# A transformer layer's ConvFFN: down projection as seven half-matrix products over all tokens, both up blocks in a row, convolution taps summed in PSUM

## The chip, the cores and the metric

The kernel runs on one core of one Trainium2 chip. The metric is the device time of one execution in microseconds (us). TensorE multiplies matrices into PSUM, VectorE (DVE), ScalarE (ACT) and GpSimd (POOL) work on vectors in SBUF, the first two also in PSUM, and SyncE (SP) mostly issues transfers. All data is float32. A matrix product is made of three TensorE passes over high and low parts of the operands (high x high, high x low, low x high), so each operand is first split: a cast gives the high part, a subtraction the low part.

## What is computed

One layer of a hybrid backbone over 2048 tokens and 256 context tokens with 1024 channels: a mixer (long convolutions, a state space scan, attention), an output projection with a norm, and then the part that the change touches, a gated feed-forward network with a short convolution along the tokens and a last norm:

```python
def _conv_ffn(h, w_up, conv_w, conv_b, w_down):
    u = _dwconv(h @ w_up, conv_w, conv_b)       # w_up: 1024 x 5632, three taps a channel
    g, val = jnp.split(u, 2, axis=-1)           # 2816 channels each
    return (jax.nn.silu(g) * val) @ w_down      # w_down: 2816 x 1024
...
x = _layernorm(ALPHA * x + gate * ffn, ln2_g, ln2_b)
```

## The kernel before

All engines run in order; the order on each engine is laid out by a scheduler when the kernel is built, which places instructions by their dependences and by estimated times. Transfers are issued from SP's queue (`nc.sync`), ScalarE's (`nc.scalar`) and GpSimd's (`nc.gpsimd`).

Everything up to the output projection is not touched, but for one thing: `outproj` takes its PSUM banks from the pool `ps_f`, of eight banks (one bank holds 128 x 512 numbers). It works through 16 tiles of 128 tokens, normalizes each, transposes it (`h2_tile`) and writes the seven input operands of the up projection (`operands`) to memory, or for the first two of them straight to SBUF.

`ffn` treats the tokens in two blocks e of 1024. For each block it runs 22 column tiles ct of the up projection, and then the down products of those token tiles that are complete.

*Up* (`up`, L1685 to L1725). The gate and value columns of a tile come from a 2 x 2 split of weights and tokens in seven products ("11", "t1", "t2", "t3", "21", "22", "t4") of twelve 128x512 matmuls each (`product`, L1657). VectorE adds the products out of PSUM into two tiles `ug` and `uv`. Three taps of the convolution follow on VectorE for each half: a scaling with bias (L1715) and two multiply-adds (L1717), all from SBUF to SBUF. ScalarE applies Silu to the gate half (L1721), VectorE multiplies the halves (L1723), and the result goes to the array `d_g[ct]` in memory. The operands stay in SBUF for a whole block in `bop`; those of the second block replace them piece by piece during the first down stage (`load_operands(1, ...)`, the iterator `side`).

*Down* (`down`, L1742 to L1770). Groups of three or four token tiles, two column halves each, so six or eight banks. For each of 22 channel tiles k the group loads its tokens from `d_g[k]`, splits them, takes the weights of row block k (two halves, split), and makes three matmuls for each tile and half (L1749 to L1751). In the second block the first eight channel tiles' weights are kept split in SBUF, in the place of the up operands. A finished tile is multiplied by the gate `g2` as it leaves PSUM (L1731), and the rest of it (`finish`, L1733: add the residual, norm, store) is put on a list `fins`, from which one is taken after each later step.

*Weights* (`weights`, L1580). One generator loads, combines and splits the weights of up and down in the order of their use, into a ring of six split operands. `split` casts on ScalarE (L1562) and subtracts in the helper `lo` (L481), mostly on GpSimd, sometimes on VectorE. `add` (L1592) combines weights on GpSimd. `take(n, more)` asks for the next n operands and prepares `more` ahead.

Of the kernel before, what the change touches and what calls it, by code (L numbers as in the profile page):

```python
# [9 lines left out]
F32 = mybir.dt.float32  # L10
# [7 lines left out]
P = 128  # L18
D = 1024
# [26 lines left out]
def shape_constants():  # L46
# [83 lines left out]
class SSD:  # L130
    """Both scans of the state space mixer, streamed over super-chunks of four chunks.  forward() yields after
    each piece of work, so that other work can be put between; the pieces of one super-chunk leave the forward
    part of y and the chunk states of the backward scan in memory, and backward() finishes from the last
    super-chunk to the first."""
# [39 lines left out]
    # step sizes and decays of chunks i0 .. i0 + n - 1  # L174
    def steps(self, i0, n):
# [7 lines left out]
        # softplus(x) = max(x, 0) + log1p(exp(-|x|))  # L183
# [17 lines left out]
        # inclusive sums within a chunk, forward heads then backward heads  # L201
# [76 lines left out]
    def off_diagonal(self, d, pr, at, hs, c_):  # L278
        """what the states hs give to the pair of heads pr over four chunks"""
# [12 lines left out]
    def rows(self, sc):  # L292
        """sums of the super-chunk as rows, split for the broadcasting products"""
# [9 lines left out]
    def forward(self, sc):  # L303
# [8 lines left out]
        # states: entering ones of the forward scan, own ones of the backward scan  # L312
# [153 lines left out]
class Build:  # L466
# [4 lines left out]
    def mm3(self, ps, pairs):  # L471
        """ps = sum over pairs of (wh, wl, xh, xl): wh.xh + wh.xl + wl.xh"""
# [23 lines left out]
    # work that runs between the pieces of other work  # L496
# [10 lines left out]
    # work that waits for a chain of other engines: run some pieces later  # L507
# [1356 lines left out]
```

## Time and profile before

| | us |
|---|---|
| median of 3 runs | 3097.09 (3082.59 to 3097.76) |
| span of the profiled execution, first to last instruction | 3087.5 |
| median less that span | 9.6 |
| output projection (from about 1500) | 213 |
| up, first block | 439.5 |
| down, first 7 token tiles | 222.5 |
| up, second block | 428.0 |
| down, last 9 token tiles | 274.5 |
| after the last matmul | 10.0 |

The stages are stretches of the profiled execution, cut where the first matmul of the next one starts; times inside it count from its first instruction. The profile lists no time of that execution other than its span, so the median of the runs is compared with the span.

### The profile page before, as it was taken

How to read it: one execution, taken by the hardware profiler on the slowest of the kernel's cores; microseconds unless marked ns; L12 is line 12 of the kernel's file. 1: busy time of each engine (PE TensorE's matmuls, PEld its weight loads, DVE VectorE, ACT ScalarE, POOL GpSimd, SP SyncE). 2: the span in 40 equal slices, each digit the busy share in tenths (PEclk: the TensorE clock that was granted, in tenths of full speed). 3: DMA queues.
4: the chain of work that ended last, by engine and by line, in shares of the span. 5: the costliest groups of instructions: out<-in, count | busy, mean ns of one | idle time of the engine just before them, and what ended most of it. 6: DMA issues, size and time to landing. Idle time of an engine off the chain costs nothing.

```text
span 3087.5 us, 41018 instructions
## 1 busy us (share of the span) xinstructions
PE 2920.1 (95%) x14153; PEld 2368.5 (77%) x14153; DVE 2198.1 (71%) x2924; ACT 1351.8 (44%) x2604; POOL 1772.2 (57%) x1418
## 2 busy tenths in 40 slices
PE   7899998899899898999999899999999999999998
PEld 4798696798866666666678788888778788888877
DVE  7953168642588977767678899999263999995344
ACT  7555135442367776667622323323333222223231
POOL 4644005300246656565564588987677899886463
PEclk9999999999999999999999999999999999999999
DMA  7467735343363329595556522223665222224563
GB/s 240 127 214 258 270 118 156 113 137 124 102 151 123 110 102 249 193 237 170 180 174 205 196 94 82 85 86 109 190 218 165 98 93 89 83 82 152 164 194 110
DMA packets 266546, 466.32 MB, mean 151 GB/s; under 512 B 32909, under 2 KB 153869, under 8 KB 262626
## 3 DMA queue, kind: packets, MB, share of 16 engines
q1 hardware_dynamic: 176656, 347.80, 36.7%
q10 hardware_dynamic: 84946, 100.55, 9.5%
q0 software_dynamic: 4736, 15.35, 1.4%
q8 instruction: 112, 1.84, 0.3%
q14 instruction: 96, 0.79, 0.1%
HBM read 325.97 MB, written 137.63 MB: 150 GB/s over the span
## 4 chain that ended last, share of the span: by engine, by line
PE 67%; DVE 13%; DMA 8%; issue 5%; ACT 4%; POOL 3%; ACTq 1%; SPq 0%; POOLq 0%; DVEq 0%
PE ps_f L1663 8%; PE ps_f L1662 8%; PE ps_f L1664 8%; PE ps_p L477 4%; PE ps_p L478 4%; PE ps_p L476 4%; PE ps_f L1750 3%; PE ps_f L1751 3%; PE ps_f L1749 3%; PE ps_f L476 2%; PE ps_f L477 2%; PE ps_f L478 2%; PE ps_o L1345 1%; PE ps_m L1305 1%; DMA kk<-d_ks 1%
## 5 line engine op out<-in xcount | busy, mean ns | idle before, releaser
L481 POOL TENSOR_TENSOR wrl<-wf,wrh 128x512 fp32r<-128x512 f32 x304 | 502.6, 1670 | 184.9 <-ACT wrh L1562 83.6
L481 POOL TENSOR_TENSOR pl<-pf,ph 128x512 fp32r<-128x512 f32 x186 | 263.3, 1424 | 197.1 <-ACT ph L1356 165.9
L1717 DVE SCALAR_TENSOR_TENSOR y<-u,cwf,y 128x1023 f32<-128x1023 f32 (+1 forms) x176 | 343.7, 1954 | 4.5
L1562 ACT CAST wrh<-wf 128x512 fp32r<-128x512 f32 x348 | 206.9, 618 | 240.7 <-PE ps_f L1663 139.5
L476 PE MATMUL ps_p<-hh,wh 128*128 128x342 f32 (+1 forms) x800 | 268.2, 335 | 0.0
L478 PE MATMUL ps_p<-hh,wl 128*128 128x342 f32 (+1 forms) x800 | 266.5, 334 | 0.0
L477 PE MATMUL ps_p<-hl,wh 128*128 128x342 f32 (+1 forms) x800 | 266.4, 333 | 0.0
L1306 DVE TENSOR_REDUCE mx<-ps_m 128x1 f32<-128x512 f32 (+1 forms) x320 | 196.1, 631 | 67.7 <-PE ps_m L1305 65.4
L481 DVE TENSOR_TENSOR wrl<-pc,wrh 128x384 fp32r<-128x384 f32 (+1 forms) x102 | 81.3, 799 | 211.4 <-ACT wrh L1616 200.8
L1562 ACT CAST wrh<-sw 128x512 fp32r<-128x512 f32 x132 | 81.2, 621 | 330.8 <-POOL sw L1592 230.4
L1750 PE MATMUL ps_f<-wrl,wrh 128*128 128x512 f32 x560 | 215.6, 394 | 5.4 <-POOL wrl L481 5.1
L1698 DVE TENSOR_TENSOR u<-ps_f,u 128x512 f32<-128x512 f32 x308 | 203.6, 684 | 17.2 <-PE ps_f L1664 11.7
L1751 PE MATMUL ps_f<-wrh,wrl 128*128 128x512 f32 x560 | 213.2, 390 | 1.9 <-DVE wrl L481 1.9
L1353 ACT ACTIVATE pf<-ps_s 128x512 f32<-128x512 f32 x288 | 168.2, 604 | 91.5 <-PE ps_s L1351 55.4
L481 DVE TENSOR_TENSOR wl<-wf,wh 128x1024 fp32r<-128x1024 f32 x36 | 48.4, 1343 | 223.5 <-ACT wh L834 223.4
L1356 ACT CAST ph<-pf 128x512 fp32r<-128x512 f32 x288 | 173.3, 629 | 20.1 <-DMA q<-d_qh 5.4
L239 POOL TENSOR_TENSOR hd<-h,dec 128x512 f32<-128x512 f32 x31 | 40.3, 1301 | 221.0 <-DVE h L248 141.3
L1749 PE MATMUL ps_f<-wrh 128*128 128x512 f32 x560 | 161.3, 390 | 0.5 <-ACT wrh L1562 0.5
L477 PEld LDWEIGHTS ps_p<-hl,wh 128*128 128x128 f32 x800 | 151.1, 189 | 11.7 <-issue 5.0
L478 PEld LDWEIGHTS ps_p<-hh,wl 128*128 128x128 f32 x800 | 150.6, 188 | 11.3 <-issue 5.0
L476 PEld LDWEIGHTS ps_p<-hh,wh 128*128 128x128 f32 x800 | 151.3, 189 | 8.8 <-issue 2.0
L1305 PE MATMUL ps_m<-k,q 128*128 128x512 f32 (+1 forms) x320 | 123.7, 400 | 14.8 <-DVE mx L1306 12.3
(475 smaller groups left out, 8718.9 us busy)
## 6 DMA issues: line engine op xcount, KB each, us to landing
wf<-in_ffn_w_down SPq DMA_DIRECT2D x94, 512.0 KB, 3.6
wf<-in_w_up SPq DMA_DIRECT2D x88, 512.0 KB, 3.5
wmod<-in_w_mod SPq DMA_DIRECT2D x24, 1024.0 KB, 7.5
wf<-in_w_col SPq DMA_DIRECT2D x36, 512.0 KB, 4.2
pc<-d_g SPq DMA_DIRECT2D x88, 192.0 KB, 3.3
kk<-d_ks SPq DMA_DIRECT2D x56, 256.0 KB, 8.9
d_g<-y SPq DMA_DIRECT2D x22, 512.5 KB, 2.6
d_g<-y SPq DMA_DIRECT2D x22, 511.5 KB, 2.7
```

Of the source, the lines that this page charges most:

```text
L476: mm(ps, lhsT=wh, rhs=xh, start=i == 0, stop=False)
L477: mm(ps, lhsT=wh, rhs=xl, start=False, stop=False)
L478: mm(ps, lhsT=wl, rhs=xh, start=False, stop=i == n - 1)
L481: eng.tensor_tensor(out=dst, in0=src, in1=hi.bitcast(F32), op=ALU.subtract)
L1562: self.nc.scalar.copy(w[0], x)
L1662: mm(ps, lhsT=w[0][:, js], rhs=b[0][:, j], start=j == 0, stop=False)
L1663: mm(ps, lhsT=w[0][:, js], rhs=b[1][:, j], start=False, stop=False)
L1664: mm(ps, lhsT=w[1][:, js], rhs=b[0][:, j], start=False, stop=j == 3)
L1717: v.scalar_tensor_tensor(y, u[:, o + k:o + k + n], cw[:, k, c:c + 1], y, op0=ALU.mult, op1=ALU.add)
L1749: mm(p, lhsT=x[0][:, ts], rhs=w[0], start=k == order[0], stop=False)
L1750: mm(p, lhsT=x[0][:, ts], rhs=w[1], start=False, stop=False)
L1751: mm(p, lhsT=x[1][:, ts], rhs=w[0], start=False, stop=k == order[-1])
```

## The change

The down projection waits until both blocks of up are done. It is then made over all 2048 tokens as seven products of half matrices: the tokens are split into two halves of 1024, the 2816 channels into two halves of 11 tiles (`KH`), the 1024 output columns into two halves of 512. A product covers eight tiles of 128 tokens (`PAIRS`), one bank each, and eleven steps k; each step needs one split weight piece of 512 columns and one split token piece of 1024. Sums and differences of pieces are formed as they are loaded. Those that are used again are stored: `d_gs` for tokens, `d_wt` for weights, both written in "t2". The last product, "t4", runs in three groups of three, three and two tiles and prepares its weights anew for each. The finishing of the first 1024 tokens is put on the list after "22", and taken from it in the steps of "t3"; that of the others after each group of "t4".

In up, the first tap of each half is made by ScalarE into a PSUM tile of two banks (`ps_c`, two such tiles), the other two taps are added there by VectorE, and Silu and the product read it. `ps_f` keeps four banks. A PSUM tile holds 1024 columns, so the last of the 1025 columns of the second block is done by itself. The operands of the second block are loaded after each product of the first block's last column tile.

```diff
-KEPT = 8
-DOWN = ((range(0, 4), range(4, 7)), (range(7, 10), range(10, 13), range(13, 16)))
+DOWN = ("11", "t2", "t1", "21", "22", "t3", "t4", "t4", "t4")
+PAIRS = (range(8), ) * 6 + (range(0, 3), range(3, 6), range(6, 8))
+KH = NFF // P // 2
...
-                self.ps_f = es.enter_context(tc.tile_pool(name="ps_f", bufs=8, space=PSUM))
                 self.ffn_start()
-                self.outproj()
-                self.ffn()
+                with tc.tile_pool(name="ps_f", bufs=4, space=PSUM) as self.ps_f:
+                    with tc.tile_pool(name="ps_c", bufs=2, space=PSUM) as self.ps_c:
+                        self.outproj()
+                        self.ffn_up()
+                self.ffn_down()
...
# weights()
-        def down(k, tiles, keep, first, last):
...
+        def down(name, k, last):
+            wd, h0, h1 = self.a["ffn_w_down"][0], slice(0, 512), slice(512, 1024)
+            r0, r1 = slice(k * P, (k + 1) * P), slice((KH + k) * P, (KH + k + 1) * P)
...
+            eng = g
+            if name == "11":
+                x = half(wd[r0, h0])
...
+            elif name == "t1":
+                x = half(self.d_wt[0][k])
+            elif name == "t2":
+                b1, x = raw(wd[r0, :]), half(wd[r1, h1])
+                add(b1[:, h1], b1[:, h1], b1[:, h0], ALU.subtract)
+                nc.sync.dma_start(self.d_wt[0][k], b1[:, h1])
+                add(x, x, b1[:, h1], ALU.subtract)
+                nc.sync.dma_start(self.d_wt[1][k], x)
+            elif name == "t3":
+                y, x = half(wd[r0, h1]), half(wd[r1, h1])
+                add(x, x, y, ALU.subtract)
+            else:
+                y, x = half(self.d_wt[1][k]), half(wd[r1, h0])
+                add(x, x, y, ALU.subtract)
+                eng = v if k % 2 else g
+            yield self.split(x, eng)
...
# up()
+                if e == 0 and ct == nf - 1:
+                    for _ in self.load_operands(1, [name]):
+                        pass
...
-                    v.tensor_scalar(y, u[:, o + 1:o + 1 + n], cw[:, 1, c:c + 1], cw[:, 3, c:c + 1], op0=ALU.mult, op1=ALU.add)
+            parts = ((0, 1023), ) if e == 0 else ((0, 1024), (1024, 1))
...
+                    if m > 1:
+                        y = self.ps_c.tile([P, 1024], F32, name="ps_c", tag="c")[:, :m]
+                    else:
+                        y = pool.tile([P, 1], F32, name="y1", tag=f"y1{i}")
+                    s.activation(y, u[:, o + 1 + p0:o + 1 + p0 + m], AF.Identity, scale=cw[:, 1, c:c + 1], bias=cw[:, 3, c:c + 1])
                     for k in (0, 2):
-                        v.scalar_tensor_tensor(y, u[:, o + k:o + k + n], cw[:, k, c:c + 1], y, op0=ALU.mult, op1=ALU.add)
+                        v.scalar_tensor_tensor(y, u[:, o + k + p0:o + k + p0 + m], cw[:, k, c:c + 1], y, op0=ALU.mult, op1=ALU.add)
...
+                s.activation(out[:, p0:p0 + m], ys[0], AF.Silu)
+                self.last = v.tensor_tensor(out=out[:, p0:p0 + m], in0=out[:, p0:p0 + m], in1=ys[1], op=ALU.mult)
...
+    def ffn_down(self):
...
+            def operands():
+                for n, name in enumerate(DOWN):
+                    c0, m = P * PAIRS[n][0], P * len(PAIRS[n])
+                    t1, t2 = slice(c0, c0 + m), slice(1024 + c0, 1024 + c0 + m)
+                    def load(src):
+                        x = self.pcpool.tile([P, 1028], F32, name="gr", tag="u", bufs=4)[:, :m]
+                        nc.sync.dma_start(x, src)
+                        return x
+                    for k in range(KH):
+                        lo_, hi_ = self.d_g[k], self.d_g[KH + k]
...
+                        elif name == "t1":
+                            x = load(self.d_gs[0][k])
+                        elif name == "t2":
+                            x, y, z = load(lo_[:, t2]), load(hi_[:, t2]), load(lo_[:, t1])
+                            v.tensor_tensor(out=x, in0=x, in1=y, op=ALU.add)
+                            nc.scalar.dma_start(self.d_gs[0][k], x)
+                            v.tensor_tensor(out=y, in0=x, in1=z, op=ALU.subtract)
+                            nc.scalar.dma_start(self.d_gs[1][k], y)
+                            x = y
+                        elif name == "22":
+                            x, y = load(hi_[:, t1]), load(self.d_gs[1][k])
+                            v.tensor_tensor(out=x, in0=x, in1=y, op=ALU.subtract)
+                        else:
+                            x, y = load(lo_[:, t1]), load(lo_[:, t2])
+                            v.tensor_tensor(out=x, in0=x, in1=y, op=ALU.subtract)
+                        w = [lp.tile([P, 1024], F32R, name="g" + e, bufs=4)[:, :m] for e in "hl"]
+                        s.copy(w[0], x)
+                        self.lo(v, w[1], x, w[0])
+                        yield w
...
+            def take():
+                while len(ops) < 3:
...
+            def evacuate(n, name, p, ps):
...
+                elif name == "22":
+                    add(xa[p][:, h1], xb[p][:, h1])
+                    fins.append(lambda: finish(p, xa[p], g))
+                elif name == "t3":
+                    add(xb[p][:, h1], xb[p][:, h1])
+                    add(xb[p][:, h0], xb[p][:, h0])
+                else:
+                    add(xb[p][:, h0], xb[p][:, h0])
+                    fins.append(lambda: finish(8 + p, xb[p], v if p > 5 else g))
+            def finish(t, r, eng):
+                x1 = lp.tile([P, D], F32, name="x1", bufs=2)
+                nc.sync.dma_start(x1, self.d_x1[t])
+                eng.tensor_tensor(out=r, in0=r, in1=g2, op=ALU.mult)
+                v.scalar_tensor_tensor(r, x1, ALPHA, r, op0=ALU.mult, op1=ALU.add)
+                self.norm(self.pcpool, r, gam, bet, r)
+                nc.scalar.dma_start(self.out[0, t * P:(t + 1) * P, :], r)
+            for n, name in enumerate(DOWN):
+                pairs = PAIRS[n]
+                ps = [ps_d.tile([P, 512], F32, name="ps_d", tag="d") for _ in pairs]
+                for k in range(KH):
+                    (w, ), x = self.take(1, 3), take()
+                    for i in range(len(pairs)):
+                        ts = slice(i * P, (i + 1) * P)
+                        mm(ps[i], lhsT=x[0][:, ts], rhs=w[0], start=k == 0, stop=False)
+                        mm(ps[i], lhsT=x[0][:, ts], rhs=w[1], start=False, stop=False)
+                        mm(ps[i], lhsT=x[1][:, ts], rhs=w[0], start=False, stop=k == KH - 1)
+                    if fins:
+                        fins.pop(0)()
+                for i, p in enumerate(pairs):
+                    evacuate(n, name, p, ps[i])
```

## Rows read from the trace of the kernel before

**Rows 1.** The page, part 1: busy time, share of the span, instructions.

```profile
PE 2920.1 (95%) x14153; PEld 2368.5 (77%) x14153; DVE 2198.1 (71%) x2924; ACT 1351.8 (44%) x2604; POOL 1772.2 (57%) x1418
```

**Rows 2.** Windows by stage: stretch, length, busy of each engine, clock, DMA, GB/s.

```profile
1713.00:2152.50 439.50, 428.74 (x1859) 350.18 (x1857) 419.88 (x387) 138.99 (x229) 358.84 (x276) 0.99 0.32 107
2152.50:2375.00 222.50, 216.46 (x930) 172.74 (x929) 93.56 (x107) 85.56 (x156) 151.13 (x109) 1.00 0.63 197
2375.00:2803.00 428.00, 422.98 (x1846) 346.11 (x1846) 412.17 (x372) 128.97 (x209) 380.94 (x293) 1.00 0.27 90
2803.00:3077.50 274.50, 272.65 (x1189) 222.22 (x1187) 114.92 (x157) 81.47 (x151) 135.68 (x100) 1.00 0.51 162
3077.50:3087.50 10.00, 0.14 (x1) 0.00 (x0) 4.92 (x7) 0.00 (x0) 1.46 (x1) 0.77 0.13 52
```

**Rows 3.** Windows of 50 us in the first up stage and the second down stage.

```profile
1700.00:1750.00 50.00, 43.41 (x185) 34.70 (x183) 38.28 (x56) 19.62 (x39) 20.97 (x21) 0.90 0.73 249
1750.00:1800.00 50.00, 46.67 (x205) 38.14 (x204) 49.25 (x44) 14.37 (x24) 37.35 (x30) 1.00 0.28 93
1950.00:2000.00 50.00, 50.00 (x220) 41.06 (x219) 48.88 (x44) 13.79 (x23) 46.28 (x34) 1.00 0.27 93
...
2900.00:2950.00 50.00, 50.00 (x220) 41.02 (x219) 16.94 (x28) 13.53 (x26) 22.40 (x17) 1.00 0.49 150
```

**Rows 4.** Timeline of VectorE, then of GpSimd, in the second up stage.

```profile
2616.52 3.52 DVE L1717 SCALAR_TENSOR_TENSOR y<-u,cwf,y 128x1025 f32<-128x1025 f32 x2
2620.14 2.14 DVE L1723 TENSOR_TENSOR y<-y 128x1025 f32<-128x1025 f32 x1
...
2604.63 1.29 POOL L481 TENSOR_TENSOR wrl<-sw,wrh 128x512 fp32r<-128x512 f32 x1
...
2616.84 4.35 POOL L481 TENSOR_TENSOR wrl<-wf,wrh 128x512 fp32r<-128x512 f32 x2 [1.01 <-ACT wrh L1562]
2621.14 1.18 POOL L1693 COPY u<-tail 128x2 f32<-128x2 f32 x1
```

**Rows 5.** Groups by line and shape, whole span: busy, mean ns of one, idle before.

```profile
L1698 DVE TENSOR_TENSOR u<-ps_f,u 128x512 f32<-128x512 f32 x308 | 203.6, 684 | 17.2 <-PE ps_f L1664 11.7
L1717 DVE SCALAR_TENSOR_TENSOR y<-u,cwf,y 128x1025 f32<-128x1025 f32 x88 | 168.9, 1921 | 2.2
L372 DVE SCALAR_TENSOR_TENSOR y<-xT,ssdc,ps_y 128x512 f32<-128x512 f32 x16 | 11.9, 745 | 7.1 <-PE ps_y L365 7.1
...
L481 POOL TENSOR_TENSOR fxl<-fax,fxh 128x1024 fp32r<-128x1024 f32 x15 | 38.2, 2545 | 12.4 <-ACT fxh L1072 6.3 <-PE ps_x L478 3.8 <-DMA d_xt<-tst 1.2
...
L1721 ACT ACTIVATE y<-y 128x1025 f32<-128x1025 f32 x22 | 23.4, 1065 | 46.9 <-DVE y L1717 46.9
```

**Rows 6.** Timeline after the last matmul: the last tile's norm.

```profile
3079.12 0.69 DVE L1427 BATCH_NORM_STATS2 bst<-r 128x6 f32<-128x512 f32 x1
...
3080.17 1.27 DVE L1434 SCALAR_TENSOR_TENSOR r<-r,bmv,gam 128x1024 f32<-128x1024 f32 x1
3080.39 1.46 POOL L1433 TENSOR_TENSOR brs<-bve,mhalf 128x1 f32<-128x1 f32 x1 [9.64 <-DVE bve L1431]
3081.89 1.28 DVE L1435 SCALAR_TENSOR_TENSOR r<-r,brs,bet 128x1024 f32<-128x1024 f32 x1 [0.45 <-POOL brs L1433]
```

**Rows 7.** Windows with the highest transfer rates; columns as in rows 2.

```profile
0.00:20.00 20.00, 11.08 (x27) 3.09 (x27) 7.77 (x19) 10.53 (x16) 7.38 (x19) 0.91 0.89 321
1720.00:1730.00 10.00, 5.24 (x12) 3.48 (x12) 7.75 (x10) 3.83 (x9) 5.26 (x5) 0.66 0.93 353
2300.00:2310.00 10.00, 6.62 (x28) 4.52 (x27) 9.68 (x12) 3.98 (x8) 7.57 (x5) 1.00 0.79 278
```

**Rows 8.** Timeline of the output projection: transposes, last evacuation, next transposes.

```profile
1618.07 1.04 PE L485 MATMUL ps_f<-ident,r 128*128 128x128 f32 x8
...
1624.86 0.46 ACT L1451 ACTIVATE h2t<-ps_f,mc 128x128 f32<-128x128 f32 x1 [0.39 <-DVE h2t L1454]
...
1629.85 1.04 PE L485 MATMUL ps_f<-ident,r 128*128 128x128 f32 x8
```

More of the change, by code (lines that the diff above doesn't have):

```diff
@@ L1638, in weights @@
                 yield from up(ct)
-            for n, tiles in enumerate(DOWN[e]):
-                for k in self.down_order(e, n):
-                    yield from down(k, tiles, e == 1 and k < KEPT, n == 0, n == len(DOWN[e]) - 1)
+        for n, name in enumerate(DOWN):
+            for k in range(KH):
+                yield from down(name, k, n == len(DOWN) - 1)
     def piece(self):
@@ L1733, in finish @@
-            def finish(t, r):
-                for b in range(2):
-                    bs = slice(b * 512, (b + 1) * 512)
-                    x1 = self.piece()
-                    nc.sync.dma_start(x1, self.d_x1[t][:, bs])
-                    v.scalar_tensor_tensor(r[:, bs], x1, ALPHA, r[:, bs], op0=ALU.mult, op1=ALU.add)
-                self.norm(pool, r, gam, bet, r)
-                nc.scalar.dma_start(self.out[0, t * P:(t + 1) * P, :], r)
-            def down(e, n, side):
-                tiles = DOWN[e][n]
-                nt, order = len(tiles), self.down_order(e, n)
-                ps = {(i, b): self.psf() for i in range(nt) for b in range(2)}
-                def products(i, b, k, x, w):
-                    mm, p, ts = nc.tensor.matmul, ps[i, b], slice(i * P, (i + 1) * P)
-                    mm(p, lhsT=x[0][:, ts], rhs=w[0], start=k == order[0], stop=False)
-                    mm(p, lhsT=x[0][:, ts], rhs=w[1], start=False, stop=False)
-                    mm(p, lhsT=x[1][:, ts], rhs=w[0], start=False, stop=k == order[-1])
-                ks = order[:nf - KEPT] if e == 1 and n == len(DOWN[1]) - 1 else order
-                for k in ks:
-                    x, *w = self.take(3, 3)
-                    for i in range(nt):
-                        for b in range(2):
-                            products(i, b, k, x, w[b])
-                    next(side, None)
@@ new lines, in ffn_up @@
+        first_operands(("21", "22", "t4"), bpool3)
+        for e in range(2):
+            for ct in range(nf):
+                for _ in first.pop(0) if first else up(e, ct):
+                    pass
+                if e == 0 and ct == 2:
+                    with tc.issue_after(self.last.ins):
+                        self.norm2 = [self.bc_row(pool, a["ln2_g"], "gam2"), self.bc_row(pool, a["ln2_b"], "bet2"),
+                                      self.bc_row(pool, self.d_mod[1:2, :], "g2")]
@@ L1772, in ffn @@
-            rs = {}
-            fins = []
-            first_operands(("t2", "t3"), bpool)
-            first = [up(0, 0), up(0, 1)]
-            next(first[0])
-            self.flush()
-            next(first[1])
-            self.oppool.release()
-            first_operands(("21", "22", "t4"), es.enter_context(tc.tile_pool(name="ffb3", bufs=1)))
-            for e in range(2):
-                for ct in range(nf):
-                    for _ in first.pop(0) if first else up(e, ct):
-                        if fins:
-                            fins.pop(0)()
-                    if e == 0 and ct == 2:
-                        with tc.issue_after(self.last.ins):
-                            gam = self.bc_row(pool, a["ln2_g"], "gam2")
-                            bet = self.bc_row(pool, a["ln2_b"], "bet2")
-                            g2 = self.bc_row(pool, self.d_mod[1:2, :], "g2")
-                side = self.load_operands(1, OPERANDS) if e == 0 else iter(())
-                for n in range(len(DOWN[e])):
-                    down(e, n, side)
-                for _ in side:
-                    pass
+                for i, p in enumerate(pairs):
+                    evacuate(n, name, p, ps[i])
```

173 lines of the change are left out of this document (99 added, 74 removed).

## The prediction

> **What bounds the kernel now.** I read the page first, then the windows by stage, then single stretches. The busy line of the page [rows 1] names the tensor engine, at 95% of the span. The windows by stage [rows 2] say where this is strictly so. In both up stages and in the second down stage it is busy for 98 to 99% of the time; in the first down stage it loses some 6 us. Full windows [rows 3] hold 220 matmuls in 50 us at clock 1.00, so one 128x512 matmul is issued every 0.2273 us (its listed 0.39 us overlaps its neighbours). Per stage that gives: the up products, 2 x 22 x 7 x 12 = 3696 matmuls, need 840 us and took 439.5 + 428 = 867.5; the down products, 16 x 2 x 22 x 3 = 2112, need 480 us and took 222.5 + 274.5 = 497, and 10 us of tail come after them, 507 in all.
>
> The second bound stands close behind it. In the up stages VectorE is busy 412 to 420 us and GpSimd 359 to 381 [rows 2], but these busy times hold waits for each other. In [rows 4] VectorE starts two convolution taps at 2616.52 and a multiply at 2620.14, and GpSimd two subtractions at 2616.84 and a copy at 2621.14. Alone, a tap takes some 1.28 us and such a subtraction 1.29 [rows 4, 6]. Together the three VectorE and two GpSimd operations take 5.76 us, from 2616.52 to 2622.28, which is 3 x 1.1 + 2 x 1.25: they take turns. So I count each VectorE operation with two SBUF inputs (1.1 us per 1024 columns, 0.55 per 512) and each GpSimd one (1.25 per 512) on one shared resource, "the turn". In the up stage one column tile needs 9 x 1.25 on GpSimd and 5 x 1.1 + 4 x 0.55 on VectorE (the two scaling operations at half price), 18.95 us, beside 84 x 0.2273 = 19.1 us of matmuls. That it fits shows that the turn can be nearly full.
>
> The Trainium skill (page "SBUF — State Buffer", section "Who interferes with whom") has this as an exclusive lock between GpSimd and VectorE instructions with two SBUF inputs, and says that a VectorE instruction with at most one SBUF input does not contend. The trace agrees on the first in [rows 4]; for the second, the adds out of PSUM stay at 684 ns while GpSimd is busy [rows 5]. By this rule the second part of the change helps VectorE, and the rest of the change, which gives both engines more two-input work, is hurt.
>
> **The change part by part.**
>
> *Fewer matmuls.* Seven half products: 7 x 8 x 11 x 3 = 1848 matmuls, 264 fewer, 60.0 us at 0.2273. 420 us remain.
>
> *Convolution taps in PSUM.* The first tap of each half goes from VectorE to ScalarE (one of 1025 columns costs 1.06 there [rows 5]), and the other four read one SBUF and one PSUM input. The nearest row is 745 ns for 512 columns with one PSUM input [rows 5], so some 1.28 for 1024; no row shows a write to PSUM, and 1.92, the present price, is the upper bound. VectorE falls from 18.9 to some 13.5 us a column tile, or 16.2 at the bound, and the turn to 12.4. Both are under 19.1, so all that can be won is what the matmuls lose today: 27 us over both stages. The windows [rows 3] put some 10 us of it before 1800, at the start, with operand loads and a clock of 0.90 that stay. I take 435 for the first block. One-column leftovers in the second block are small and stand under cover.
>
> *Four banks instead of eight.* The output projection shares the four. Its transposes at 1618.07 are evacuated by 1625.3, and the next ones, which would need the same banks, come at 1629.85 [rows 8]: 4 us to spare, cost 0 (up to 5 if VectorE falls behind). In the up stage four products are 10.9 us of cover against a conv burst of some 6.5.
>
> *Both up blocks in a row.* The 28 operand pieces of the second block, until now hidden in down, load within the last column tile of the first: 28 x 0.26 + 1.05 MB = 8.4 MB in 19 us, 440 GB/s, where the best 10 us window moved 353 [rows 7]; 24 us at that rate. I take 8 us (0 to 20). The second block: 428. Up 863, 4.5 less than now.
>
> *Into down.* All eight banks are wanted, four of them are the convolution's, which ends some 6 us after the last product; the matmuls reach the fifth bank after 2.7 us. 4 us (0 to 8).
>
> *The seven products.* Each step k has 24 matmuls, 5.45 us; a product, 60.0. "11", "t1", "21" and "22" put at most 1.31 MB (240 GB/s) and 3.5 us of turns on a step, so 60 each, 240 in all.
>
> *"t2", transfers.* A step loads three pieces of 0.524 MB, stores two, loads 0.79 MB of weights and stores 0.52: 3.93 MB, 43.3 MB in eleven steps. In 60 us that would be 720 GB/s, twice anything in [rows 7]. Read ahead ends at three operands, about 16 us or 5.5 MB. The rest at 353 GB/s is 107 us, and the last piece still needs a subtraction, a cast, a split and its matmuls, 10 us: 117. At 321, the best of 20 us, it is 128. Only four raw buffers serve three pieces a step, so the third load waits for the split of the step before; that chain (split 2.5, load 4, subtraction 1.3, waits) is 9 us a step, just under the 10.3 of the transfers, and on top of them in part would make 13 a step, 143: my upper end. The turn, 3 x 1.1 + 3 x 1.25, is 7.05 a step and hidden. The stores of the weight differences stand in SP's queue and wait for GpSimd's subtractions, with the next loads behind them; those of the token sums stand in ScalarE's queue and wait for VectorE, with the next casts behind. Both delays are part of that chain.
>
> The Trainium skill's page "DMA: Bandwidth & Descriptors" (section "Specifications") gives a fabric ceiling of 435 GB/s. By that figure this product would take 97 us, an estimate, and the sum would be 20 less; no row here comes near the rate, so the row stands.
>
> *"t3" and "t4", turns.* A step of "t3" has a subtraction and a split of 1024 on VectorE and of 512 on GpSimd, 4.7 us; eight finishing chains fall into it. Each now multiplies by the gate on GpSimd (1024 columns, 2545 ns in [rows 5]; alone on the turn 2.5) where today the evacuation did it out of PSUM, and has three full-width VectorE passes, 3.3: 5.8 us of turn. 11 x 4.7 + 8 x 5.8 = 98 us against 60 of matmuls. "t4" runs in three groups that prepare the same eleven weights each time: 1.25 + 0.93 + 0.42 = 2.6 us a step (2.46 in the last), 84 us (0.93 is the mean of six splits on GpSimd and five of 0.55 on VectorE, 0.42 the tokens' split of 384 columns), and six chains, 35: 119 against 60. Then two chains in a row on VectorE, each 1.28 x 3 for multiply and residual and first norm pass, 1.4 of statistics, 1.28 at the end [rows 6], and the store: 19 us where today's tail is 10. Together 236. At the lower bound the turns are free and VectorE's own time counts: in "t3" 22 passes of 1.22, 16 adds out of PSUM of 0.684 and eight chains of 5.6 (three passes, statistics 1.4, small ones 0.4), 83; in "t4" splits 27, adds 5.5, chains 34, 67; 83 + 67 + 19 = 169. At the upper, a tenth of the turns is lost in waits: 258.
>
> **Sum.** Down 4 + 240 + 117 + 236 = 597 against 507, +90; up -4.5. The profiled span of 3087.5 becomes 3173; the median of the runs is 9.6 above that span, so 3183.
>
> **Rivals.** (1) *The tensor engine sets the pace*, the other side. For it: the second down stage loses under 5 us in 274 [rows 2, 3] with nine finishing chains and all splits beside it. Against it: its matmul step had a third of the side work. Down is then 4 + 420 + 19, the time 3097 - 64 - 4.5 = 3029. It decides once the waits in "t2", "t3" and "t4" together, 57 + 97 in my sum, fall under 70. (2) *Turns are mostly hidden*: the lower bound 169 in the last two products, everything else as summed: 3116. (3) *Chains add up*: "t2" at 143, a tenth lost in turns, and the clock, which fell to 0.66 in a window with 5.2 us of matmuls in 10 but stayed 1.00 with 6.6 [rows 7], falls where matmuls pause, at some 10 us: 3097 + 85.5 + 26 + 22 + 10 = 3240.
>
> **Chances.** My forecast, between 3145 and 3215: 0.58. Rival 1: 0.08. Rival 2, 3100 to 3145: 0.14, a fifth of it within 0.5%. Rival 3: 0.20. About 0.5% (15 us) is what a measurement of this kernel can tell from no change. Faster 0.08, same 0.05 with the edges, slower 0.87. The range, 3112 to 3250, leaves out rival 1 and the top of rival 3.
>
> **What would show it.** Right: matmuls at 19.1 us a column tile in up, VectorE at some 70% there; in "t2" the matmuls half idle, behind a split that waits for a load, with over 300 GB/s; in the last two products both VectorE and GpSimd over 85% busy, and taps near 1.3 us. Wrong: "t2" near 60 us; GpSimd's 1024-wide multiply beside VectorE's passes without either stretching; or an up stage that the four banks hold above 19.5 us a tile.

## The result, and the profile after

The changed kernel takes 3206.7 us (median of 4 runs, 3200.55 to 3216.45) where the kernel before takes 3093.4 in the runs beside it: ratio 1.0375, 95% interval 1.0344 to 1.0405. It is slower by 113 us; the prediction was 3183, range 3112 to 3250. The profiled execution's span went from 3087.5 to 3198.7 us.

The page, part 1, for the changed kernel (the same line as [rows 1]):

```profile
PE 2917.5 (91%) x13889; PEld 2349.9 (73%) x13889; DVE 2137.2 (67%) x3004; ACT 1463.5 (46%) x2666; POOL 1584.2 (50%) x1394
```

The tensor engine has 264 instructions fewer, and yet its busy time fell by only 2.6 us. Its granted clock is 0.86, 0.87 and 0.76 in the windows of "t2", "t3" and "t4" below, a mix of its two levels (1.2 and 2.4 GHz), and each of these stretches holds long waits; where it has no waits, as in "t1", the clock is 1.00. No engine has more to do than before, but for ScalarE. So the time went into waits, and the windows by stage show where. They are cut at the first matmul of each step: output projection, first up block, second up block, the entry into down, "11", "t2", "t1", "21", "22", "t3", "t4", tail. Columns as in [rows 2].

```profile
1510.90:1717.30 206.40, 192.14 (x897) 159.66 (x895) 154.12 (x211) 51.44 (x90) 108.06 (x88) 0.96 0.53 181
1717.30:2159.30 442.00, 430.38 (x1859) 351.09 (x1858) 295.94 (x347) 198.13 (x280) 276.49 (x287) 0.99 0.32 108
2159.30:2593.00 433.70, 426.88 (x1849) 347.98 (x1847) 337.80 (x425) 205.93 (x324) 274.40 (x291) 0.99 0.27 91
2593.00:2604.80 11.80, 0.19 (x1) 0.01 (x1) 11.10 (x12) 6.77 (x8) 1.27 (x1) 0.73 0.87 291
2604.80:2666.90 62.10, 61.97 (x265) 50.84 (x265) 17.79 (x14) 15.54 (x22) 27.79 (x20) 0.97 0.74 259
2666.90:2767.20 100.30, 73.42 (x265) 56.62 (x265) 39.61 (x31) 22.33 (x31) 36.87 (x24) 0.86 0.96 352
2767.20:2827.20 60.00, 60.00 (x265) 49.68 (x266) 21.94 (x25) 17.15 (x23) 19.82 (x11) 1.00 0.50 168
2827.20:2892.20 65.00, 59.95 (x265) 49.35 (x264) 22.18 (x20) 18.76 (x24) 20.14 (x12) 1.00 0.47 159
2892.20:2959.30 67.10, 61.64 (x264) 50.59 (x264) 34.39 (x30) 16.30 (x21) 21.49 (x15) 0.96 0.68 231
2959.30:3054.90 95.60, 72.56 (x264) 56.49 (x265) 94.86 (x87) 16.89 (x24) 76.74 (x38) 0.87 0.66 230
3054.90:3181.50 126.60, 86.66 (x264) 56.40 (x264) 96.05 (x106) 28.47 (x56) 85.13 (x53) 0.76 0.60 196
3181.50:3198.70 17.20, 0.35 (x2) 0.00 (x0) 13.27 (x18) 0.00 (x0) 2.78 (x2) 0.62 0.15 61
```

Each product has the same 264 matmuls and could be done in 60.0 us; only "t1" is. "t2" has the transfer engines taken for 0.96 of its time, "t3" has VectorE busy for 99% of it, and in "t4" no engine is above 76%. Against the sum of the prediction, term by term in us:

| term | predicted | measured | difference |
|---|---|---|---|
| output projection (four banks) | 0 | 197.0 before, 205.3 after | +8.3 |
| up, first block, second block with the transition | 435 + 428 | 442 + 434 | +13 |
| into down | 4 | 11.8 | +7.8 |
| "11", "t1", "21", "22" | 240 | 62.1 + 60.0 + 65.0 + 67.1 = 254 | +14 |
| "t2" | 117 | 100.3 | -17 |
| "t3" | 98 | 95.6 | -2 |
| "t4" | 119 | 126.6 | +8 |
| tail | 19 | 17.2 | -2 |

These differences sum to +30; the work ahead of the output projection ended 4 us earlier in the profiled execution after, and the two make the 26 between the 3173 summed and the 3198.7 found. (The output projection's times run from the start of its first product to the start of its last, without the transposes that follow.)

### The profile page after: what moved, and what is told of

It is laid out like the page before. It is cut to its first block, busy times and chain, and to the rows that moved or that the text cites. A ratio compares the mean times of both kernels' runs of the same rounds, so it can differ in the third digit from the quotient of the medians.

```text
span 3198.7 us, 40745 instructions
## 1 busy us (share of the span) xinstructions
PE 2917.5 (91%) x13889; PEld 2349.9 (73%) x13889; DVE 2137.2 (67%) x3004; ACT 1463.5 (46%) x2666; POOL 1584.2 (50%) x1394
## 4 chain that ended last, share of the span: by engine, by line
PE 64%; DVE 13%; DMA 11%; issue 5%; POOL 3%; ACT 3%; SPq 0%; ACTq 0%; DVEq 0%; POOLq 0%
PE ps_f L1679 8%; PE ps_f L1678 8%; PE ps_f L1680 8%; PE ps_p L479 4%; PE ps_p L478 4%; PE ps_p L477 4%; DMA gr<-d_g 2%; DMA wf<-in_ffn_w_down 2%; PE ps_f L478 2%; PE ps_f L477 2%; PE ps_f L479 2%; DMA kk<-d_ks 2%; PE ps_d L1883 2%; PE ps_d L1884 2%; PE ps_o L1350 1%
## 5 line engine op out<-in xcount | busy, mean ns | idle before, releaser
L482 POOL TENSOR_TENSOR wrl<-wf,wrh 128x512 fp32r<-128x512 f32 x216 | 308.4, 1428 | 400.0 <-ACT wrh L1563 379.3
L1882 PE MATMUL ps_d<-wrh,gh 128*128 128x512 f32 x616 | 256.1, 427 | 73.8 <-ACT gh L1827 30.8
L1883 PE MATMUL ps_d<-wrl,gh 128*128 128x512 f32 x616 | 260.5, 423 | 23.2 <-DVE wrl L482 12.4
L1751 DVE SCALAR_TENSOR_TENSOR ps_c<-u,cwf,ps_c 128x1023 f32<-128x1023 f32 (+1 forms) x176 | 224.3, 1285 | 58.5 <-ACT ps_c L1749 57.0
L1884 PE MATMUL ps_d<-wrh,gl 128*128 128x512 f32 x616 | 235.3, 407 | 15.1 <-DVE gl L482 9.2
L1827 ACT CAST gh<-gr 128x1024 fp32r<-128x1024 f32 (+2 forms) x99 | 84.4, 858 | 303.0 <-PE ps_d L1883 175.5
L1882 PEld LDWEIGHTS ps_d<-wrh,gh 128*128 128x128 f32 x616 | 125.4, 207 | 115.6 <-ACT gh L1827 40.0
L1593 POOL TENSOR_TENSOR wf<-wf 128x512 f32<-128x512 f32 x110 | 162.4, 1476 | 92.6 <-DMA wf<-in_ffn_w_down 74.7
L482 DVE TENSOR_TENSOR gl<-gr,gh 128x1024 fp32r<-128x1024 f32 (+2 forms) x99 | 127.2, 1292 | 117.1 <-ACT gh L1827 117.1
L1883 PEld LDWEIGHTS ps_d<-wrl,gh 128*128 128x128 f32 x616 | 126.6, 206 | 60.7 <-DVE wrl L482 17.2
```

The lines of the kernel that those rows point to most:

```text
L482: eng.tensor_tensor(out=dst, in0=src, in1=hi.bitcast(F32), op=ALU.subtract)
L1751: v.scalar_tensor_tensor(y, u[:, o + k + p0:o + k + p0 + m], cw[:, k, c:c + 1], y, op0=ALU.mult, op1=ALU.add)
L1882: mm(ps[i], lhsT=x[0][:, ts], rhs=w[0], start=k == 0, stop=False)
L1883: mm(ps[i], lhsT=x[0][:, ts], rhs=w[1], start=False, stop=False)
L1884: mm(ps[i], lhsT=x[1][:, ts], rhs=w[0], start=False, stop=k == KH - 1)
```

## The experiments

Runs for which no ratio is given were executed once. The four executions of the changed kernel lie 16 us apart, so such runs are read by their stages, which repeat better: in the seven runs that leave "t2" as it is, it takes 99.6 to 103.8 us.

### What sets the pace of "t2": bytes or the four raw buffers

**Six raw buffers.** Every third load goes to a buffer of a second pair.

```diff
-x = self.pcpool.tile([P, 1028], F32, name="gr", tag="u", bufs=4)[:, :m]
+turn[0] += 1
+if turn[0] % 3:
+    x = self.pcpool.tile([P, 1028], F32, name="gr", tag="u", bufs=4)[:, :m]
+else:
+    x = lp.tile([P, 1024], F32, name="gr2", bufs=2)[:, :m]
```

> The changed kernel with six raw token buffers in the down stage where it has four (every third load goes to a buffer of a second pair), so that the loads of a step needn't wait for the split of the step before. In the changed kernel the second product, t2, takes 100.3 us at 376 to 378 GB/s. If the chain load, split, next load sets its pace, it falls by 15 to 20 us, to 80 to 85 (the turn's own floor is 77), and the whole to about 3185. If the transfers set it, as the prediction has it (43 MB at the rate that the queues reach), t2 stays within 4 us of 100 and the whole within 6 of 3204.

**No stores.** The changed kernel without the four stores of "t2".

```diff
-nc.sync.dma_start(self.d_wt[0][k], b1[:, h1])
...
-nc.sync.dma_start(self.d_wt[1][k], x)
...
-nc.scalar.dma_start(self.d_gs[0][k], x)
...
-nc.scalar.dma_start(self.d_gs[1][k], y)
```

> The changed kernel without the four stores of the second product (token sums, token differences, two halves of weight differences); the later products read other arrays of the same size instead, so their operands are not those of the reference. A step of t2 then moves 2.36 MB where it moved 3.93. If the bytes set t2's pace, it falls from 100.3 us to the larger of the turn (11 x 7.05 = 77) and the bytes at 376 GB/s (69): about 77, and the whole to about 3181. If the chain of four raw buffers sets it, it stays above 92. Products t1, 21 and 22 stay at 60, 65 and 67 under either.

**Both together.**

> The changed kernel with six raw token buffers (t2 81.8 us in the run six_raw, with 404 to 418 GB/s) and without the four stores of t2 (68.3 in the run no_stores; later products read other arrays, so their operands are not the reference's). Products 11 and t2 together took 162.4 in the changed kernel, 144.3 with six buffers, 136.2 without stores. If the 144.3 are set by bytes, taking away 17 MB of 43 brings t2 near its matmuls: 60 to 66, 11 and t2 together 122 to 128. If the turn (77 us of VectorE and GpSimd work) sets them, t2 stays at 72 to 78 and the two together above 133.

Six buffers: 3183.7 us, "t2" 81.8, where the theory of the chain said 80 to 85. No stores: 3182.3, "t2" 68.3, below what either theory said; "11" took 67.9 in that run, the two together 136.2. Both: 3161.4, "t2" 59.8, the two together 122.1. (The expectations' 376 to 378 GB/s is the rate over 82 us from 2654.5 on; over "t2" itself it is 352.) Windows of 10 us in "t2" of the changed kernel, which show that the queues are full at first and not at the end:

```profile
2660.00:2670.00 10.00, 9.89 (x44) 7.84 (x44) 2.85 (x3) 5.94 (x11) 5.59 (x4) 1.00 1.03 406
2700.00:2710.00 10.00, 7.95 (x23) 6.31 (x24) 4.25 (x4) 1.66 (x2) 5.16 (x4) 0.66 1.03 406
2730.00:2740.00 10.00, 7.19 (x31) 5.29 (x29) 4.13 (x4) 1.57 (x2) 1.81 (x1) 1.00 0.85 299
```

"t2" as one window, with six buffers:

```profile
2670.00:2752.00 82.00, 68.94 (x267) 54.63 (x266) 34.16 (x27) 20.05 (x26) 38.49 (x25) 0.90 1.03 412
```

and with six buffers and no stores:

```profile
2668.00:2728.00 60.00, 60.00 (x266) 49.70 (x265) 48.19 (x28) 20.37 (x29) 45.44 (x25) 1.00 0.96 339
```

With six buffers the queues run at 412 GB/s through the whole product; with four they fall to 299 in its second half. So neither theory was whole. Of the 40 us over the matmuls, 18 belong to the chain through four raw buffers (100.3 - 81.8), and 22 to the stores (81.8 - 59.8), 17 of the 43 MB. In the other order the shares differ: without the stores the chain costs 14, "11" and "t2" taken together, 5.7 of them a wait for the first bank of "t2". The edit also takes the stores' waits out of SP's and ScalarE's queues, so that the 22 are bytes alone is not shown; the steady 412 GB/s speaks for it. In the last run "t2" stands at its matmuls although the prediction counts 77 us of turns for it. That is no proof against turns: in this window lie 27 passes of VectorE with two SBUF inputs and 25 operations of GpSimd, 61 us at the prediction's prices, and seven of the 22 additions and subtractions of "t2" were done in "11".

### What sets the pace of "t3": the finishing chains and their turns

**No gate.** The gate multiply of each chain is left out.

```diff
-eng.tensor_tensor(out=r, in0=r, in1=g2, op=ALU.mult)
```

> The changed kernel without the multiplication by the gate in the finishing of a tile (the output lacks the gate). Fourteen of the sixteen are GpSimd operations over 1024 columns, eight of them in t3. Theory of turns (GpSimd and two-input VectorE work exclude each other): taking GpSimd work away speeds VectorE, which does not do it, by 2.5 us each: t3 falls from 95.6 us by 15 to 20, t4 and the tail together from 141.6 by 15 to 20, the whole to about 3170. Rival, VectorE's own work alone sets the pace: its passes stay as long as they are, t3 stays within 5 us, and the whole falls by less than 8 us, of which 3 are the last two tiles, gated on VectorE.

**No finishing chains of the first half.** The raw sums are stored.

```diff
-fins.append(lambda: finish(p, xa[p], g))
+nc.scalar.dma_start(self.out[0, p * P:(p + 1) * P, :], xa[p])
```

> The changed kernel without the finishing chains of the first half (gate, residual, norm of eight token tiles): the raw sums are stored in their place. The same loads, subtractions and splits of t3 remain, and their turns are 11 x 4.7 = 52 us, so by the prediction's turns t3 becomes bound by its 60 us of matmuls: 60 to 64 instead of 95.6, the whole about 3173. Rival: t3 is held by its own operands (two loads and a subtraction a step, four raw buffers, the same chain as in t2); then t3 stays above 80 and the whole above 3190.

Without the gate: 3176.6 us, "t3" 84.0 instead of 95.6, "t4" 116.0 instead of 126.6, the tail 15.0. Both falls, 11.6 and 12.8, are less than the 15 to 20 that the theory of turns gave, and more than its rival's 5. Without the chains: 3176.1 us, "t3" 63.2, with the same loads, subtractions and splits. The window of that "t3":

```profile
2964.50:3027.70 63.20, 61.72 (x265) 50.58 (x266) 36.22 (x36) 16.02 (x23) 31.51 (x20) 0.98 0.81 283
```

The eight chains are what holds "t3", and eight multiplies that stand on another engine are worth 11.6 us of it; by VectorE's own time alone they would be worth nothing. The groups of "t3" in the changed kernel show how (busy, mean of one, idle before):

```profile
L1870 DVE SCALAR_TENSOR_TENSOR xa<-x,xa 128x1024 f32<-128x1024 f32 x8 | 17.6, 2198 | 0.0
L482 DVE TENSOR_TENSOR gl<-gr,gh 128x1024 fp32r<-128x1024 f32 x9 | 15.6, 1730 | 0.0
L1825 DVE TENSOR_TENSOR gr<-gr 128x1024 f32<-128x1024 f32 x7 | 13.6, 1936 | 0.7 <-DMA gr<-d_g 0.7
...
L1869 POOL TENSOR_TENSOR xa<-xa,g 128x1024 f32<-128x1024 f32 x8 | 24.8, 3131 | 0.0
```

VectorE's operations with two SBUF inputs take 1.73 to 2.20 us where the prediction had 1.22, and GpSimd's multiply 3.13 where its nearest row had 2.545 [rows 5]. With the two norm passes (2.02 and 1.67) these means lie some 28 us in sum above what the same operations take alone, so that much of VectorE's 94.9 busy us is waiting inside its instructions. In the run without the gate VectorE is busy for 83.3 of the 84.0 us with the same operations, and those with two SBUF inputs are shorter, while the statistics, with one, stay at 675 ns. The window of that "t3", and two of its groups:

```profile
2959.90:3043.90 84.00, 68.91 (x265) 53.38 (x265) 83.31 (x87) 15.99 (x24) 50.41 (x30) 0.92 0.79 267
...
L1869 DVE SCALAR_TENSOR_TENSOR xa<-x,xa 128x1024 f32<-128x1024 f32 x8 | 13.2, 1646 | 0.7 <-DMA x<-d_x 0.7
L1825 DVE TENSOR_TENSOR gr<-gr 128x1024 f32<-128x1024 f32 x7 | 11.5, 1649 | 0.0
```

**Every other step.** The last product in one group (below), and a chain taken only at odd steps.

```diff
-if fins:
+if fins and k % 2:
```

> The changed kernel with the last product in one group of eight pairs (as in the run t4_one: 3181 us, t3 96.5) and one change more: the finishing chains that fall into t3 are taken only every other step, so that they spread over the product. The same chains are there in number, so where turns set t3's pace, it stays near 96 us for all chains that it still holds: with five of its eight chains in t3 and three left for t4, t3 falls by 3 x 5.8 = 17 to about 80, t4 takes three chains more under its 60 us of matmuls with 11 x 2.6 = 29 of turns and 17 of chains, so it stays near 61; the whole 3165. If what holds t3 up is instead the VectorE alone, a chain costs 5.6 there and the same move gives the same 17. If t3 is held by something that doesn't go with the chains (loads of the token halves, the clock), t3 stays above 92 and the whole at 3180.

3181.6 us, ratio to before 1.0283 (1.0258 to 1.0307); "t3" 97.5, and no shorter. It tells nothing about the theories: in its trace all eight residual additions still start between 7.9 and 62.9 us after the start of "t3" (9.8 to 61.9 in the run with one group alone). The order that the scheduler laid out left the chains where they had been. The run without chains settles what this one couldn't.

### "t4" and the tail

**One group.** The eight pairs of the last product in one group; its weights are prepared once.

```diff
-DOWN = ("11", "t2", "t1", "21", "22", "t3", "t4", "t4", "t4")
-PAIRS = (range(8), ) * 6 + (range(0, 3), range(3, 6), range(6, 8))
+DOWN = ("11", "t2", "t1", "21", "22", "t3", "t4")
+PAIRS = (range(8), ) * 7
```

> The changed kernel with t4 as one group of eight tiles in place of three, three and two. Theory: t4 is held back by preparing its weights three times (2.6 us of turns a step against 2.04 us of matmuls, 33 steps) and by six finishing chains in its last two groups. One group has 11 steps of 3.3 us of turns under 60 us of matmuls, and then eight finishing chains in a row of 5.6 to 6.2 us on VectorE, 45 to 50, and the store: 60 + 50 + 5 = 115 from the start of t4 to the end against 141.6 now, the whole near 3180. Rival, the three groups hide most of the finishing and the eight chains at the end cost all that is won: 140 us or more, the whole at 3205 or above.

3181.2 us, ratio 1.0279 (1.026 to 1.0298), 25 us better than the changed kernel: "t4" 61.2 and the tail 54.5, 116 together, where the three groups took 126.6 + 17.2 = 144. All eight chains now follow the last matmul, and that is still cheaper than preparing eleven weights three times. The window of its tail:

```profile
3126.00:3181.00 55.00, 1.13 (x5) 0.59 (x4) 50.54 (x61) 0.00 (x0) 27.00 (x13) 0.54 0.36 134
```

### The entry into down

**Waits by tile.** The eight banks of down wait each for its own former user instead of all together.

```diff
-ps_d = es.enter_context(tc.tile_pool(name="ps_d", bufs=8, space=PSUM))
+ps_d = es.enter_context(tc.tile_pool(name="ps_d", bufs=8, space=PSUM, reuse_waits="tile"))
```

> The changed kernel with the eight banks of the down products waiting for each earlier tile by itself instead of for the whole earlier pool. Theory: the 11.6 us that the first down matmul waits for the last multiplication of the convolution are a wait of the pool, since its bank held an up product that was read long before. Then the first three or four tiles start at once and the wait is 4 to 6 us; the whole falls by 5 to 7 us. Rival: the first bank of the down products is itself one of the convolution's, and the wait stays at 11 to 12 us.

3204.7 us, inside the spread of the changed kernel. The first down matmul starts 1.9 us after the last one of up, where it was 12, but "11" then takes 71.6 us instead of 62.1. The waits of the tensor engine in it:

```profile
PE ps_d L1882 <- DVE y L1754: 5.8, 1, 5.8
PE ps_d L1884 <- DVE gl L482: 2.7, 1, 2.7
PE ps_d L1882 <- ACT gh L1827: 1.5, 1, 1.5
```

The wait only moved: after three matmuls, at its second bank, the tensor engine waits for the convolution's last multiplication (L1754), which ends as late as before. The timeline of VectorE in the changed kernel after up's last matmul at 2592.80 (start, length) has the reason:

```profile
2595.55 1.27 DVE L1751 SCALAR_TENSOR_TENSOR ps_c<-u,cwf,ps_c 128x1024 f32<-128x1024 f32 x1
...
2596.87 2.35 DVE L482 TENSOR_TENSOR gl<-gr,gh 128x1024 fp32r<-128x1024 f32 x2
2599.14 1.28 DVE L1751 SCALAR_TENSOR_TENSOR ps_c<-u,cwf,ps_c 128x1024 f32<-128x1024 f32 x1
...
2602.32 1.23 DVE L482 TENSOR_TENSOR gl<-gr,gh 128x1024 fp32r<-128x1024 f32 x1 [0.58 <-ACT gh L1827]
2603.46 1.21 DVE L1754 TENSOR_TENSOR y<-y,ps_c 128x1024 f32<-128x1024 f32 x1
```

The last multiply ends at 2604.7, 11.9 us after the last product and not the 6 that the prediction allowed, for three splits of the next stage, 3.6 us, stand between the taps.

### Convolution and banks alone

**The second part of the change in the kernel before.** Taps in PSUM, four banks and two tiles of two; down as it was, but that its groups take the double tiles for their third and fourth token tiles.

```diff
-self.ps_f = es.enter_context(tc.tile_pool(name="ps_f", bufs=8, space=PSUM))
+self.ps_f = es.enter_context(tc.tile_pool(name="ps_f", bufs=4, space=PSUM))
+self.ps_c = es.enter_context(tc.tile_pool(name="ps_c", bufs=2, space=PSUM))
...
+s.activation(y, u[:, o + 1 + p0:o + 1 + p0 + m], AF.Identity, scale=cw[:, 1, c:c + 1], bias=cw[:, 3, c:c + 1])
+for k in (0, 2):
+    v.scalar_tensor_tensor(y, u[:, o + k + p0:o + k + p0 + m], cw[:, k, c:c + 1], y, op0=ALU.mult, op1=ALU.add)
```

> The kernel before with only the second part of the change: the first tap on ScalarE into PSUM, the other two added there, four banks for products and two double banks for the taps; the down groups use the double banks for their third and fourth tiles. Theory: matmuls set the pace of up at 19.2 us a column tile before and after, so only the stalls of the first tiles of each block can be won: the second block falls from 428 to about 423, the first stays within 5 us of 439.5, and the output projection loses up to 8 us with four banks. The whole lies between 8 us below and 8 us above the kernel before. Rival, VectorE's relief is worth what it was short of in up (27 us over 840): 3070 or below.

3107.0 us against 3090.8: ratio 1.0053 (1.0039 to 1.0066), slower by 16 us and outside the 8 either way that were expected. The output projection takes 205.0 instead of 197.0, and the second block's first column tile 35.1 instead of 22.0. In that tile the tensor engine waits 13.6 us for an addition of VectorE that empties a bank, while VectorE works off finishing chains of the first down stage; with eight banks it ran ahead. In the changed kernel no down stage stands between the blocks, so these 13 us are not part of its loss; the 8 of the output projection are. From the third tile on the other tiles take 19.2 to 19.3 us, and nearly all took 19.2 before.

**The rows through another queue.** The output projection's 8 us were looked for in the order of SP's queue. In the changed kernel it stands so (the third load of `mf` waits for its buffer):

```profile
1497.31 28.81 SPq L1505 DMA_DIRECT2D mf<-d_m  x3
1526.18 0.58 SPq L1424 DMA_DIRECT2D gam<-in_ln_g  x1
1526.85 1.58 SPq L1424 DMA_DIRECT2D bet<-in_ln_b  x1
1528.53 0.45 SPq L1424 DMA_DIRECT2D g<-d_mod  x1
```

and in the kernel before, the first of those rows:

```profile
1512.58 0.35 SPq L1419 DMA_DIRECT2D gam<-in_ln_g  x1
```

VectorE then waits 9.6 us for `g`, and the tensor engine 14.2 us for the first norm, where it waited 8.5.

```diff
-self.nc.sync.dma_start(t, src.to_broadcast([P, D]))
+eng = self.nc.scalar if name in ("gam", "bet", "g1") else self.nc.sync
+eng.dma_start(t, src.to_broadcast([P, D]))
```

> The changed kernel with one edit: the broadcast rows that the output projection's first norm needs are loaded through ScalarE's queue instead of SP's, where in the trace after they stand behind a load that waits 28.8 us for its buffer. If that order is why the output projection takes 8 us more than before, its second tile falls from 26.9 to 13 to 20 us, the stage from 205 to about 197, and the whole by 8 us to about 3198. If the four banks themselves cost the 8 us, the second tile stays near 27 and the whole at 3206.

3216.1 us, ratio 1.0394 (1.0372 to 1.0417): no better. On ScalarE's queue the three loads stand behind a cast that waits for the tensor engine. They start 12.6 to 13.5 us after the stage's first matmul, where it was 15.3 to 17.6, and in the kernel before 1.5 to 2.5 ahead of it. VectorE no longer waits for `g`; but its order changed too, and now a split that waits 9.7 us for a cast stands ahead of the additions that need `g`. The second tile took 32.8 us instead of 26.9. So this run doesn't test the order. That the rows come 14 us later and that VectorE waits for one of them is seen in the trace; that four banks cost nothing once the rows are early was not shown, and stays open.

### The two best edits together

> The changed kernel with the two edits that gained most by themselves: six raw buffers (t2 100.3 to 81.8) and the last product in one group (t4 and tail 143 to 116). They lie in different stretches, so they add: 3207 - 18 - 25 = 3164, ratio to before 1.023. If t4's loads or t3 collide with the two more buffers, it stays above 3172.

> As six_t4, and the gate multiply of the finishing chains left out (so the output is not the reference's): a bound on what moving the gate elsewhere could give. Without the gate alone, t3 went from 95.6 to 84.0, and the chains of t4 lost some; t3 is then at the VectorE's own 83. Expected: six_t4 less 11 in t3, and 0 to 8 in the tail, where the gate of eight chains stands beside VectorE: 3145 to 3153. Still above the kernel before (3094): the three costs together are 57 of the 113 us.

Six buffers and one group: 3146.0 us, ratio 1.0162 (1.014 to 1.0184), 18 us better than expected. Most of the surplus is in "t3", which falls from 96.5 to 84.1 us; the run with six buffers alone had 89.0 there already, and the expected sum took only its "t2". With six raw buffers more is done ahead: five of the eleven subtractions lie inside "t3" (seven with four buffers), and three of the chains' sixteen norm passes now lie behind it. The two groups of subtractions:

```profile
L1831 DVE TENSOR_TENSOR gr<-gr,gr 128x1024 f32<-128x1024 f32 x3 | 6.8, 2257 | 0.0
...
L1831 DVE TENSOR_TENSOR gr<-gr 128x1024 f32<-128x1024 f32 x2 | 3.4, 1684 | 0.0
```

Without the gate as well: 3127.9, 18 us less, within the 11 to 19 expected of the step, but not as it was split: "t3" gives 6 (78.2) and the tail 11.5 (43.0). It is the fastest variant, leaves a multiply out, and is still 32 us slower than the kernel before (3096 in the runs beside it). No run points to a version of this change that beats it.

## Why the prediction held, step by step

**Right by mechanism, and in the sum: "t3", "t4" and the tail.** They were summed to 236 and took 239, and it is the turns that make "t3": taking one GpSimd multiply out of each of eight chains gave 11.6 us (the lower bound, VectorE's own time, would have given none), taking the chains out gave all but 3 us back. The single prices are less exact than their total. The eight multiplies stand in the sum at 20 us and were worth 11.6, and 6 with six buffers; and only seven of the eleven subtractions lie in "t3". The sum forecasts the stretch, not what a part is worth. In "t4" the sum is near (119 and 126.6) but the mechanism is only half of it: VectorE is at 76% and GpSimd at 67%, not above 85 as foretold (in "t3" they are at 99 and 80), and the tensor engine's waits are split between casts (16.7 us), VectorE's splits (12.4) and GpSimd's (10.7): a chain of load, combination, cast and split that three short groups can't run ahead of. The gate's share there, 10.6 us, is less than the 15 that six turns of 2.5 give.

The Trainium skill's page "SBUF — State Buffer", section "Who interferes with whom", says that a VectorE instruction with at most one SBUF input, outside the modes that use both ports, doesn't contend with GpSimd. The trace agrees: the taps with one input in PSUM take 1285 ns where those from SBUF took 1921 [rows 5], and the additions out of PSUM stay at 688 (684 before).

**Right by sign, wrong in size: "t2".** Its term was "the rest at 353 GB/s is 107 us". The best window of [rows 7] was taken for a ceiling, and it is not even the best in the trace of the kernel before, which moves more while it loads its first weights:

```profile
25.00:35.00 10.00, 3.57 (x12) 1.27 (x13) 6.11 (x13) 7.86 (x15) 0.00 (x0) 0.65 1.02 416
```

The changed kernel moves 406, and with six buffers 412 over the whole product. What the prediction counted as lying under the transfers, the chain of four raw buffers, is 18 of the 40 us. So 100.3 is 82 at the full rate and 18 of the chain, not 107 of bytes and 10 of latency. At 416 GB/s the prediction's own sum would give 91 and 10, near the 100.3 with the chain still left out, by luck. (A step's 3.93 MB at 353 GB/s take 11.1 us, not the 10.3 that it sets against the chain's 9.) The page "DMA: Bandwidth & Descriptors" of the Trainium skill (section "Specifications") with its ceiling of 435 GB/s was the better guide: the highest windows of 10 us here stand at 416 to 418. The limit of about 358 GB/s that the same section gives for a core is half of what two cores of a memory stack share; these runs use one core, and go above it.

**Missed: the costs put at nothing.** Four costs put at little or nothing all came out higher, 43 us together.
- The *four banks* "cost 0 (up to 5)" by a look at the transposes alone. The output projection took 8 us more, with the change in the order of SP's queue that goes with it; the part alone did the same in the kernel before.
- In *up* the first block was to gain 4.5 and lost 2.4: nearly every tile but the first two already stood at 19.2 us, so VectorE's fall from 419.9 us busy [rows 2] to 295.9 had no place to show. The second block lost 6: its transition took 10 us instead of 8, and its tiles 19.2 to 19.3 us instead of 19.1. The one-column leftovers, called small, show 59 us on VectorE (88 of 675 ns), but under cover.
- *Into down*: 11.8 instead of 4. The prediction let the first four banks start at once, but the down products wait for all former users together; and the convolution ends 11.9 us after the last product instead of 6, 3.6 of it for splits of the next stage between the last taps.
- The *seams* of the products were not in the sum at all. "21" and "22" each end with a wait of the tensor engine for a bank, 5.1 and 5.5 us of the 14 that the four short products took too long. Before the first of them VectorE's timeline reads:

```profile
2890.24 1.23 DVE L1822 TENSOR_TENSOR gr<-gr 128x1024 f32<-128x1024 f32 x1 [4.39 <-DMA gr<-d_gs]
2891.39 0.68 DVE L1847 TENSOR_TENSOR xa<-ps_d,xa 128x512 f32<-128x512 f32 x1
```

The addition that empties the first bank stands behind a subtraction for the next product that waits 4.4 us for its load; all eight banks are in use, so nothing can start. This is read from the trace; no run changes that order.

**The offset.** The 9.6 us between span and median are no property of the measurement: each execution on record lasts 1.7 to 2.0 us longer than its own span (the profiled one 3200.55 and 3198.7). The rest is the spread between executions. That it fitted again, with 8.0, is luck.

**The rivals.** The tensor engine as the pace (3029) fell at once: the waits in "t2", "t3" and "t4" are 40 + 36 + 67 us, twice its limit of 70. Hidden turns (3116) fell with the run without the gate. Chains that add up (3240) has a part in the truth, since buffers and seams cost 18 + 11, but "t2" stayed 43 us below its 143. That the whole came within 24 us is in part luck, errors that cancel: 17 too much in "t2" against 43 too little at the seams and the edges.

## What to carry to other kernels

Fewer matmuls pay only if what feeds a product fits beside it: here 60 us of matmuls were saved, and 143 us of waits for loads, buffers, turns and weights came up in three of the seven products. A sum of turns was a good forecast for a whole stretch here, and a poor one for what removing one operation gives. A transfer rate read from a trace is a lower bound on what the queues can do, not a ceiling, so look for the highest one over the whole span, and cost a stage that asks for more by both that rate and the buffers in flight. And when a stage is cut into products that use all banks, write down for every seam which instruction frees the first bank and what stands ahead of it on its engine; three seams here cost 5 to 12 us each that no sum of busy times shows.

## What the runs showed of the hardware

The 16 transfer engines moved 412 GB/s over 82 us, loads and stores mixed, with 418 in the best of the windows of 10 us. A share of busy time near 1 is not a rate: the changed kernel had 0.96 at 352 GB/s in "t2". GpSimd's multiply of 128x1024 beside VectorE's passes took 3.13 us on average, and VectorE's two-input passes 1.7 to 2.2 beside it; in the entry into down, where GpSimd is busy for 1.3 of 11.8 us, they took 1.2. A tap of a single column on VectorE took 675 ns on average beside GpSimd, and 205 at the least. ScalarE's first tap (a scaling with bias) of 1024 columns into PSUM took 1210 ns, where its Silu of 1025 columns within SBUF took 1065 [rows 5].
